# Up-projection of a two-layer decoder trunk: seven block products in place of eight on four K blocks of eight strip pairs per layer

## The chip, the cores and the metric

One NeuronCore of one Trainium2 chip runs the whole program. The metric is the device time of one execution in microseconds (us), lower being better. Below, PE is TensorE, DVE is VectorE, ACT is ScalarE, POOL is GpSimd and SP is SyncE; SP only starts transfers here, and POOL starts those of the turns described below.

## What is computed

The reference is a decoder trunk of two layers on 256 tokens of width 2048, all in float32. Each layer is an attention (stick-breaking in the first, dilated windows over a shared K and V in the second), then a gated feed-forward block, then a gated addition of a per-layer embedding. The change is in the feed-forward block only:

```python
def conv_ffn(h, w_up, conv_w, conv_b, w_down):
    u = causal_depthwise_conv(h @ w_up, conv_w, conv_b)
    gate, val = u[..., :D_FF], u[..., D_FF:]
    return (jax.nn.silu(gate) * val) @ w_down
```

Here `D_FF` is 5632, so `w_up` is 2048 by 11264, and the convolution runs over three tokens within a column.

## The kernel before

**Products.** Weights are cut into strips of 512 columns. K, the 2048 rows of `w_up`, is cut into 16 blocks of 128. A strip's product for the 256 tokens is two accumulators of 128 tokens by 512 columns, each one PSUM bank. Each block takes three matmuls for each accumulator, since both operands are held as a high and a low part: x low by w high, x high by w low, x high by w high (`add_block`, L336). So a strip is 16 blocks x 2 halves of the tokens x 3 = 96 matmuls of 128x512.

**Weights.** `weights` (L274) lets SP load four blocks at a time (one `raw` buffer, 1 MB, four such buffers in the pool). Two blocks together, a tile of 1024 columns, are then split: ACT writes the high part `whi` (L302), DVE subtracts it from the raw weights and writes `wlo` (L303). There are four buffers each of `whi` and `wlo`, so the splits can run up to four tiles ahead of PE. PE uses a tile in 12 matmuls.

**The feed-forward block.** `ffn` takes the up-projection in two parts per layer: strips 0 to 4, then a part of the down-projection, then strips 5 to 10, then the rest of the down-projection. Each strip s is a pair: the gate strip s and the value strip s + 11 (`products`, L356, called at L803). When a strip's accumulators are complete, ACT scales them out of PSUM (`scaled`, L406), DVE transposes 32 by 32 squares (L240), POOL sends the result through DRAM to finish the turn (L243, L251), and one strip later ACT and DVE do the convolution, the gate, and the split for the down-projection (L771 to L793, L147, L148).

**Order.** The order on each engine is fixed when the program is built: a scheduler places the instructions by priority, and every engine then takes its own list strictly in that order, waiting on semaphores. Weight splits are recorded with a higher priority (`high_priority`) so that they stand early. Matmuls stand in the order in which the code is written.

Of the kernel before, what the change touches and what calls it, by code (L numbers as in the profile page):

```python
# [26 lines left out]
FB = FF // P  # L27
# [45 lines left out]
def tile_trunk(ctx, tc, head_d, xT_d, x_d, pT_d, pos_d, vec_d, cst_d, csb_d, wqkv, wo_a, wkv, wq_b, wo_b, wup, wdn, wpg, wpp, gfin_d, out_d):  # L73
    nc = tc.nc
# [156 lines left out]
    def four(s):  # L231

        return tt(s, (P, 4 * S), tag="four", bufs=3)
# [84 lines left out]
    def strip_v(W, s, xs, base=0, tail=2, ringed=0, begun=None, ends=True, before=lambda k0: None, room=None, halved=False, ready=None):  # L318

        n = len(xs)
        ps = begun or [None] * (2 + halved)
        it = ready or weights(W, s, n, before=before, base=base, ringed=ringed)
        it = steps(it, n, 2 + halved, tail if ends else 0)
        for k, o, hi, lo in (g for group in it for g in group):
            if ps[o] is None:
                ps[o] = bank("accv", "acc") if room is None else room[:, o]
                if halved and o:  # L330
                    ps[o] = ps[o][:, :S]
            c = slice((o - 1) * S, o * S) if halved and o else slice(0, 512)
# [3 lines left out]
    def add_block(ps, x, t, hi, lo, first, final):  # L336
        xh = x[:, t * P : (t + 1) * P]
        xl = x[:, S + t * P : S + (t + 1) * P]
        nc.tensor.matmul(ps, xl, hi, start=first, stop=False)  # L339
        nc.tensor.matmul(ps, xh, lo, start=False, stop=False)  # L340
        nc.tensor.matmul(ps, xh, hi, start=False, stop=final)  # L341

    def two_strips(W, strips, xs, before, block):

# [11 lines left out]
    def products(jobs, xs, late=None, at=0, then={}, side=2):  # L356

        jobs = list(jobs)
        if late is not None:
            n = len(xs)

            def add():
                with tc.issue_after(last["high"]), tc.issue_after(last["low weights"]):
                    late()

            def before(k0):
                if k0 == at:
# [16 lines left out]
            ready = None  # L389
            if at is None:  # L390
                W, s, base = jobs[0]
                ready = list(weights(W, s, 4, base=base + n))
                add()
            for b, (W, s, base) in zip(begun, jobs):
                yield strip_v(W, s, xs[n:], base + n, begun=b, ready=ready)
                ready = None
            jobs = jobs[side:]
        for W, s, base in jobs:
            yield strip_v(W, s, xs, base)

    def scaled(ps, rc, room):

# [357 lines left out]
    def ffn(i, xs, late, rc):  # L760
        cv = V_CONV + i * 4 * 2 * FB

        def taps(r, j, n=1):
            c = cv + r * 2 * FB + j
            return vec[:, c : c + n]

        def conv_turned(j, z, y):

            runs = y.rearrange("p o (a r) -> p o a r", r=32)
            for o in range(4):  # L770
                nc.scalar.activation(runs[:, o], z[:, :, o], AF.Identity, scale=taps(2, j + o), bias=taps(3, j + o))  # L771
                for d in (1, 2):
                    c = runs[:, o, :, d:]
                    nc.vector.scalar_tensor_tensor(c, z[:, :, o, : 32 - d], taps(2 - d, j + o), c, op0=OP.mult, op1=OP.add)  # L774
            for d in (1, 2):
                over = tt("over", (P, 7, 4, 2), bufs=2)[:, :, :, :d]
                w = taps(2 - d, j, 4).unsqueeze(1).unsqueeze(3).to_broadcast([P, 7, 4, d])
                nc.vector.tensor_tensor(over, z[:, :7, :, 32 - d :], w, op=OP.mult)
                c = y.rearrange("p o (a r) -> p a o r", r=32)[:, 1:, :, :d]
                nc.vector.tensor_tensor(c, c, over, op=OP.add)  # L780

        def part(strips, late=None):

            gs = []
            gate = [None]

            def finish_strip(value, s, z):
                y = four("val" if value else "gate").rearrange("p (o c) -> p o c", o=4)
                conv_turned(4 * s + value * FB, z, y)
                if not value:  # L790
                    gate[0] = y
                    return nc.scalar.activation(y, y, AF.Silu).ins
                nc.vector.tensor_tensor(y, y, gate[0], op=OP.mult)  # L793
# [23 lines left out]
        half = FB // 4 // 2  # L817
        gs, late, _ = part(range(half), late)
# [221 lines left out]
```

## Time and profile before

| what | value |
|---|---|
| median of 3 runs | 2302.58 us (2302.34 to 2302.81) |
| span of the profiled execution | 2298.6 us |
| PE busy | 2286.6 us (99%), 10197 matmuls recorded |
| weight loads of PE (PEld) | 1893.6 us (82%) |
| DVE busy | 1514.4 us (66%) |
| ACT busy | 1257.3 us (55%) |
| POOL busy | 328.4 us (14%) |
| HBM traffic | 233 GB/s over the span |

The page of the profile gives one execution. The profiled execution's own time is known only as its span, from the first to the last instruction; the median of the runs lies 4.0 us above it. A group of instructions is written as line, engine, operation, output<-input, count, busy time and mean time of one; the last column is the time that the engine stood idle just ahead of such instructions, and what ended that wait. An engine's busy share counts instructions that are under way, so for PE, whose matmuls overlap, starts say more than durations.

### The profile page before, as it was taken

What the parts mean: (1) busy time and instruction counts of PE and PEld (TensorE: products, weight loads), DVE (VectorE), ACT (ScalarE), POOL (GpSimd) and SP (SyncE); (2) the same over time, 40 slices, a digit from 0 to 9 for tenths busy, and PEclk for the clock granted to TensorE, in tenths of its full rate; (3) what the DMA queues carried; (4) which work ended last, traced back from release to release, by engine and by line L of the source; (5) the groups of instructions that cost most, each with busy time, mean ns of one, the idle gap of its engine ahead of it and who ended that gap; (6) DMA issues with size and microseconds to landing.
All of it is one profiled execution on the core that took longest, in us unless ns stands there. A gap on an engine that the chain in (4) does not pass through costs nothing.

```text
span 2298.6 us, 27859 instructions
## 1 busy us (share of the span) xinstructions
PE 2286.6 (99%) x10197; PEld 1893.6 (82%) x10197; DVE 1514.4 (66%) x2205; ACT 1257.3 (55%) x1680; POOL 328.4 (14%) x575
## 2 busy tenths in 40 slices
PE   9999999999999999999999999999999999999998
PEld 7888888888888888888888888888888888888887
DVE  7666666676754767765677665767675476776565
ACT  6554555655534555644565554565553465554554
POOL 0311111111100111101111331211110011110100
PEclk9999999999999999999999999999999999999999
DMA  8777667767656677767577776777765577776763
GB/s 308 254 236 250 221 240 249 247 239 246 223 199 208 241 245 240 244 205 246 205 263 240 252 262 216 262 253 242 237 237 188 215 237 243 244 238 211 239 226 119
DMA packets 98346, 538.44 MB, mean 234 GB/s; under 512 B 16672, under 2 KB 17568, under 8 KB 46752
## 3 DMA queue, kind: packets, MB, share of 16 engines
q1 hardware_dynamic: 63360, 435.46, 54.2%
q0 software_dynamic: 32560, 95.98, 14.0%
q10 hardware_dynamic: 2288, 5.21, 0.6%
q8 instruction: 80, 1.31, 0.2%
q14 instruction: 58, 0.48, 0.1%
HBM read 486.52 MB, written 50.07 MB: 233 GB/s over the span
## 4 chain that ended last, share of the span: by engine, by line
PE 97%; DMA 1%; ACT 1%; DVE 0%; issue 0%; POOL 0%; SPq 0%; ACTq 0%; DVEq 0%; POOLq 0%
PE accv L340 32%; PE accv L341 31%; PE accv L339 31%; PE two L420 1%; PE two L341 0%; PE two L340 0%; PE two L339 0%; DMA turned<-there 0%; DMA there<-y 0%; PE keys L420 0%; ACT whi L302 0%; DVE wlo L303 0%; DMA vec<-in_head 0%; ACT h L140 0%; POOL turned L251 0%
## 5 line engine op out<-in xcount | busy, mean ns | idle before, releaser
L303 DVE TENSOR_TENSOR wlo<-raw,whi 128x1024 fp32r<-128x1024 f32 (+1 forms) x824 | 1001.7, 1216 | 696.0 <-ACT whi L302 694.9
L302 ACT ACTIVATE whi<-raw 128x1024 fp32r<-128x1024 f32 (+1 forms) x824 | 867.8, 1054 | 910.4 <-PE accv L341 886.7
L341 PE MATMUL accv<-whi,h 128*128 128x512 f32 x2328 | 905.3, 389 | 0.0
L339 PE MATMUL accv<-whi,h 128*128 128x512 f32 x2328 | 904.1, 388 | 0.9 <-ACT whi L302 0.6
L340 PE MATMUL accv<-wlo,h 128*128 128x512 f32 x2328 | 904.6, 389 | 0.1
L339 PEld LDWEIGHTS accv<-whi,h 128*128 128x128 f32 x2328 | 437.0, 188 | 92.0 <-ACT whi L302 1.3
L340 PEld LDWEIGHTS accv<-wlo,h 128*128 128x128 f32 x2328 | 437.0, 188 | 91.5 <-DVE wlo L303 1.4
L341 PEld LDWEIGHTS accv<-whi,h 128*128 128x128 f32 x2328 | 437.1, 188 | 89.6
L243 POOL DMA_DIRECT2D there<-y x162 | 91.7, 566 | 1305.5 <-DVE y L240 1288.5
L339 PE MATMUL accv<-whi,g 128*128 128x512 f32 x704 | 273.9, 389 | 0.0
L340 PE MATMUL accv<-wlo,g 128*128 128x512 f32 x704 | 273.9, 389 | 0.0
L341 PE MATMUL accv<-whi,g 128*128 128x512 f32 x704 | 273.9, 389 | 0.0
L251 POOL DMA_DIRECT2D turned<-there x324 | 190.0, 593 | 430.2 <-DMA there<-y 208.0
L339 PEld LDWEIGHTS accv<-whi,g 128*128 128x128 f32 x704 | 132.1, 188 | 27.5
L341 PEld LDWEIGHTS accv<-whi,g 128*128 128x128 f32 x704 | 132.1, 188 | 27.5
L340 PEld LDWEIGHTS accv<-wlo,g 128*128 128x128 f32 x704 | 132.1, 188 | 27.3
L240 DVE STREAM_TRANSPOSE y<-u 128x512 f32<-128x512 f32 x122 | 85.4, 703 | 1.8 <-DMA there<-y 1.4
L339 PE MATMUL accv<-whi,o 128*128 128x512 f32 x200 | 78.0, 390 | 0.0
L341 PE MATMUL accv<-whi,o 128*128 128x512 f32 x200 | 77.9, 390 | 0.0
L340 PE MATMUL accv<-wlo,o 128*128 128x512 f32 x200 | 77.8, 389 | 0.0
L406 ACT ACTIVATE u<-accv,rcol 128x512 f32<-128x512 f32 x102 | 69.2, 678 | 13.7 <-PE accv L341 13.7
L774 DVE SCALAR_TENSOR_TENSOR val<-turned,vec,val 128x248 f32<-128x248 f32 (+1 forms) x176 | 72.2, 462 | 0.0
(163 smaller groups left out, 1179.6 us busy)
## 6 DMA issues: line engine op xcount, KB each, us to landing
raw<-in_wup SPq DMA_DIRECT2D x176, 1024.0 KB, 5.1
raw<-in_wdn SPq DMA_DIRECT2D x88, 1024.0 KB, 4.8
there<-y POOLq DMA_DIRECT2D x171, 256.0 KB, 5.0
turned<-there POOLq DMA_DIRECT2D x324, 128.0 KB, 4.8
raw<-in_wqkv SPq DMA_DIRECT2D x40, 1024.0 KB, 6.6
raw<-in_wpg SPq DMA_DIRECT2D x32, 1024.0 KB, 4.8
raw<-in_wkv SPq DMA_DIRECT2D x24, 1024.0 KB, 5.3
raw<-in_wo_a SPq DMA_DIRECT2D x16, 1024.0 KB, 5.2
```

The source lines that it names most:

```text
L240: last["turned"] = nc.vector.transpose(y.rearrange("p (b o r) -> p o b r", b=4, o=4), strip.rearrange("p (o b c) -> p o b c", o=4, b=4)).ins
L243: nc.gpsimd.dma_start(there[t * P : (t + 1) * P], y)
L251: nc.gpsimd.dma_start(z[32 * b : 32 * b + 32].rearrange("p a o r -> p a (o r)"), back[b])
L302: last["high"] = nc.scalar.activation(hi[:, c], r, AF.Copy).ins
L303: last["low weights"] = nc.vector.tensor_tensor(lo[:, c], r, f32(hi[:, c]), op=OP.subtract).ins
L339: nc.tensor.matmul(ps, xl, hi, start=first, stop=False)
L340: nc.tensor.matmul(ps, xh, lo, start=False, stop=False)
L341: nc.tensor.matmul(ps, xh, hi, start=False, stop=final)
L406: last["out"] = nc.scalar.activation(u, ps[t], AF.Copy, scale=rc[:, t : t + 1]).ins
L420: run.append(nc.tensor.matmul(*args, skip_group_check=True, **kw).ins)
L774: nc.vector.scalar_tensor_tensor(c, z[:, :, o, : 32 - d], taps(2 - d, j + o), c, op0=OP.mult, op1=OP.add)
```

## The change

Strips 2, 3, 4 and 6 to 10 of each layer (eight gate-and-value pairs, 16 in the program) take their first four K blocks in another way. Take these four blocks as two rows of two blocks, the tokens as two halves, and the pair's two strips as two columns. Then the part of the product that they make is a 2x2 by 2x2 product of blocks, with each block product six matmuls. The plain way takes eight such products, 48 matmuls. The change takes seven, 42 matmuls, of sums and differences of blocks (the Winograd form of Strassen's scheme), and combines them.

- `block_sums`, once per layer, makes the four sums of token blocks and splits them: on DVE four adds and four subtractions of 256 columns and two splits of 512, on ACT two copies of 512.
- `Seven` handles a pair. `load` fetches the four blocks of both strips into two `raw` buffers. The seven products (`first` to `seventh`) each split a 1024-column weight operand as a plain tile is split (L445 and L446), so a pair has 7 splits for 4. The weight sums are four in-place adds on DVE (L439). ACT copies two accumulators to SBUF (L478, L485), and DVE makes four sums of 512 columns in PSUM (L495 to L498).
- The first four products of a pair are put among the tiles of the value strip of the pair before, in front of tiles 1, 3, 5 and 7 of eight, or 1, 2, 4 and 5 of six, counted from 0. The last three stand in the pair's own gate strip, in front of tiles 0, 1 and 3 of six.
- The accumulators c11 and c21 of the gate strip are the two banks of the tile `two`, of which there is one; c12 and c22 of the value strip are `seven`.
- The ring of 512-column buffers grows from 40 to 42.

The new lines count in the file after the change, in which the old L302 and L303 are L305 and L306, L339 to L341 are L342 to L344, L406 is L540, L771 to L793 are L905 to L927, L147 and L148 are L150 and L151, and L240 is L243.

```diff
+HEADS8, HEADS6, TAILS = (1, 3, 5, 7), (1, 2, 4, 5), (0, 1, 3)
...
-NRING, NRAW, NWSP = 40, 4, 4
+NRING, NRAW, NWSP = 42, 4, 4
...
+        def add(self, out, a, b):
+            with tc.high_priority(offset=AHEAD):
+                nc.vector.tensor_tensor(out, a, b, op=OP.add)
+
+        def parts(self, r):
+            hi = wsp.tile([P, 2, 512], F32R, tag="hi", name=nm("whi"))
+            lo = wsp.tile([P, 2, 512], F32R, tag="lo", name=nm("wlo"))
+            with tc.high_priority(offset=AHEAD):
+                last["high"] = nc.scalar.activation(hi, r, AF.Copy).ins
+                last["low weights"] = nc.vector.tensor_tensor(lo, r, f32(hi), op=OP.subtract).ins
+            return hi, lo
...
+        def first(self):
+            gates = two_banks()
+            self.c11, self.c21 = gates[:, 0], gates[:, 1]
+            self.c12, self.c22 = (bank("seven", "acc") for _ in range(2))
...
+            w = self.parts(self.b11)
+            self.t, self.u = self.b11, self.b12
+            self.add(self.t, self.b11, self.b12)
+            self.add(self.u, self.b12, self.b22)
+            self.product(self.c11, self.token(0, 0), w, True)
+            with tc.high_priority(offset=AHEAD):
+                nc.scalar.activation(self.p, self.c11, AF.Copy)
...
+        def fourth(self):
+            w = self.parts(self.t)
+            self.add(self.t, self.t, self.b21)
+            self.product(self.c22, self.sums[2], w, True)
+            with tc.high_priority(offset=AHEAD):
+                nc.vector.tensor_tensor(self.p, self.c22, self.p, op=OP.add)
+                nc.vector.tensor_tensor(self.c21, self.c21, self.p, op=OP.add)
+                nc.vector.tensor_tensor(self.c22, self.q, self.c21, op=OP.subtract)
+                nc.vector.tensor_tensor(self.c12, self.c12, self.p, op=OP.subtract)
+
+        def fifth(self):
+            self.product(self.c11, self.token(2, 0), self.parts(self.b21))
+
+        def sixth(self):
+            self.product(self.c21, self.token(2, 1), self.parts(self.t))
+
+        def seventh(self):
+            self.product(self.c12, self.sums[3], self.parts(self.b22))
...
+    def strip_among(W, s, xs, hooks, begun=None, base=0):
+        n = len(xs) - base
+        ps = begun or [bank("accv", "acc") for _ in range(2)]
+        it = weights(W, s, n, base=base)
+
+        def tiles():
+            for i in range(n // 2):
+                if i in hooks:
+                    hooks[i]()
+                yield next(it)
+
+        for k, o, hi, lo in (g for group in steps(tiles(), n, 2) for g in group):
+            add_block(ps[o], xs[base + k], o, hi, lo, k == 0 and not begun, k == n - 1, begun is not None)
+        return ps
...
-            ups = products([(wup[i], s + v * FB // 4, 0) for s in strips for v in range(2)], xs, late, None)
...
+                    base = 4 if now else 0
+                    tiles = (len(xs) - base) // 2
+                    yield strip_among(W, s, xs, now.go_on() if now else {}, now and [now.c11, now.c21], base)
+                    yield strip_among(W, v, xs, after.begin(tiles) if after else {}, now and [now.c12, now.c22], base)
+                    now = after
```

**The order at the border of two pairs.** On PE, where the value strip of strip 2 of the first layer ends and the gate strip of strip 3 begins, there stood before (with what each waits for):

```order
L339 MATMUL accv_3972<-whi_4081,h_3297 128x512
L340 MATMUL accv_3972<-wlo_4082,h_3297 128x512
L341 MATMUL accv_3972<-whi_4081,h_3297 128x512
L339 MATMUL accv_3972<-whi_4081,h_3300 128x512
L340 MATMUL accv_3972<-wlo_4082,h_3300 128x512
L341 MATMUL accv_3972<-whi_4081,h_3300 128x512
L339 MATMUL accv_4139<-whi_4135,h_2694 128x512 [waits Activation_49]
L340 MATMUL accv_4139<-wlo_4136,h_2694 128x512 [waits DVE_49]
L341 MATMUL accv_4139<-whi_4135,h_2694 128x512
```

The same place on PE after the change, where `seven_3643` is the value strip's second accumulator, `two_4051` the next pair's c11 and c21, and the L455 rows are the fifth product:

```order
L343 MATMUL seven_3643<-wlo_4174,h_3318 128x512
L344 MATMUL seven_3643<-whi_4173,h_3318 128x512
L455 MATMUL two_4051<-whi_4225,h_2700 128x512 [waits DVE_49,Activation_49]
L455 MATMUL two_4051<-wlo_4226,h_2700 128x512
L455 MATMUL two_4051<-whi_4225,h_2700 128x512
L455 MATMUL two_4051<-whi_4225,h_2703 128x512
L455 MATMUL two_4051<-wlo_4226,h_2703 128x512
L455 MATMUL two_4051<-whi_4225,h_2703 128x512
L342 MATMUL two_4051<-whi_4237,h_2862 128x512 [waits Activation_49]
```

The next strip's first matmul used to wait for its split weights alone. The fifth product's first matmul also waits for DVE, and the count in that wait is reached only with L497, the last of the four sums in PSUM. The fourth product, whose result these sums need, stands 12 matmuls (the value strip's last tile) ahead of the fifth.

DVE at this place before, from the gate of the strip that was turned last (L793):

```order
L793 TENSOR_TENSOR val_3922<-val_3922,gate_3748 128x1024
L303 TENSOR_TENSOR wlo_4066<-raw_4063,whi_4065 128x1024
L148 TENSOR_TENSOR g_3942<-val_3922,g_3942 128x256
L148 TENSOR_TENSOR g_3943<-val_3922,g_3943 128x256
L148 TENSOR_TENSOR g_3944<-val_3922,g_3944 128x256
L148 TENSOR_TENSOR g_3945<-val_3922,g_3945 128x256
L303 TENSOR_TENSOR wlo_4082<-raw_4063,whi_4081 128x1024
L303 TENSOR_TENSOR wlo_4136<-raw_4133,whi_4135 128x1024
```

And after the change; `wlo_4226` is the low part for the fifth product, `wlo_4254` that for the sixth, `seven_4053` the fourth product's result c22, `seven_4052` c12 and `two_4051` c21:

```order
L446 TENSOR_TENSOR wlo_4226<-raw_4029,whi_4225 128x1024
L927 TENSOR_TENSOR val_3992<-val_3992,gate_3824 128x1024
L306 TENSOR_TENSOR wlo_4238<-raw_4235,whi_4237 128x1024
L495 TENSOR_TENSOR part_4054<-seven_4053,part_4054 128x512
L446 TENSOR_TENSOR wlo_4254<-raw_4029,whi_4253 128x1024
L496 TENSOR_TENSOR two_4051<-two_4051,part_4054 128x512
L498 TENSOR_TENSOR seven_4052<-seven_4052,part_4054 128x512
L497 TENSOR_TENSOR seven_4053<-part_4054,two_4051 128x512
L306 TENSOR_TENSOR wlo_4264<-raw_4235,whi_4263 128x1024
L151 TENSOR_TENSOR g_4012<-val_3992,g_4012 128x256
```

The four sums have been put into DVE's list with the split `wlo_4254` between the first and the second of them. That split needs `whi_4253`, which goes into the buffer that the fourth product's weights held, so ACT can begin it only when the fourth product is done. The place reads alike at all 16 pairs.

More of the change, by code (lines that the diff above doesn't have):

```diff
@@ L334, in strip_v, with add_block @@
         return ps
-    def add_block(ps, x, t, hi, lo, first, final):
+    def add_block(ps, x, t, hi, lo, first, final, again=False):
         xh = x[:, t * P : (t + 1) * P]
         xl = x[:, S + t * P : S + (t + 1) * P]
-        nc.tensor.matmul(ps, xl, hi, start=first, stop=False)
-        nc.tensor.matmul(ps, xh, lo, start=False, stop=False)
-        nc.tensor.matmul(ps, xh, hi, start=False, stop=final)
+        nc.tensor.matmul(ps, xl, hi, start=first, stop=False, skip_group_check=again)
+        nc.tensor.matmul(ps, xh, lo, start=False, stop=False, skip_group_check=again)
+        nc.tensor.matmul(ps, xh, hi, start=False, stop=final, skip_group_check=again)
     def two_strips(W, strips, xs, before, block):
@@ L399, in products, with block_sums @@
             yield strip_v(W, s, xs, base)
+    def block_sums(xs):
+        f = four("whole").rearrange("p (k c) -> p k c", k=4)
+        for k in range(4):
+            nc.vector.tensor_tensor(f[:, k], f32(xs[k][:, :S]), f32(xs[k][:, S:]), op=OP.add)
+        (a11, a21), (a12, a22) = ((f[:, k : k + 2, :P], f[:, k : k + 2, P:]) for k in (0, 2))
+        m = four("sums").rearrange("p (q i c) -> p q i c", q=4, i=2)
+        nc.vector.tensor_tensor(m[:, 0], a21, a22, op=OP.subtract)
+        nc.vector.tensor_tensor(m[:, 1], a11, a21, op=OP.subtract)
+        nc.vector.tensor_tensor(m[:, 2], m[:, 0], a11, op=OP.subtract)
+        nc.vector.tensor_tensor(m[:, 3], m[:, 2], a12, op=OP.add)
+        out = []
+        for q in (0, 2):
+            hi, lo = (rt("sum", dt=F32R) for _ in range(2))
+            src = m[:, q : q + 2].rearrange("p q i c -> p (q i c)")
+            nc.scalar.activation(hi, src, AF.Copy)
+            nc.vector.tensor_tensor(lo, src, f32(hi), op=OP.subtract)
+            for j in range(2):
+                out.append([[t[:, (2 * j + i) * P : (2 * j + i + 1) * P] for t in (hi, lo)] for i in range(2)])
+        return out
@@ new lines, in tile_trunk, with __init__, product, load @@
+    class Seven:
+        def __init__(self, W, s0, s1, xs, sums):
+            self.strips = W, s0, s1
+            self.sums = sums
+            self.token = lambda k, t: [[xs[k + i][:, c + t * P : c + (t + 1) * P] for c in (0, S)] for i in range(2)]
+        def add(self, out, a, b):
[8 more added lines that the diff above has]
+            return hi, lo
+        def product(self, ps, left, w, first=False):
+            for i in range(2):
+                xh, xl = left[i]
+                hi, lo = w[0][:, i], w[1][:, i]
+                for j, (x, y) in enumerate(((xl, hi), (xh, lo), (xh, hi))):
+                    begins, ends = first and i == j == 0, first and i == 1 and j == 2
+                    nc.tensor.matmul(ps, x, y, start=begins, stop=ends, skip_group_check=True)
+        def load(self):
+            W, s0, s1 = self.strips
+            raws = []
+            for s in (s0, s1):
+                raw = wraw.tile([P, RAW, 512], F32, tag="raw", name=nm("raw"))
+                nc.sync.dma_start(raw, W[s, 0])
+                raws.append(raw)
+            (self.b11, self.b21), (self.b12, self.b22) = ((r[:, :2], r[:, 2:]) for r in raws)
+        def first(self):
+            gates = two_banks()
+            self.c11, self.c21 = gates[:, 0], gates[:, 1]
+            self.c12, self.c22 = (bank("seven", "acc") for _ in range(2))
+            both = tt("part", (P, 1024), tag="e", bufs=1)
+            self.p, self.q = both[:, :512], both[:, 512:]
+            w = self.parts(self.b11)
[5 more added lines that the diff above has]
+                nc.scalar.activation(self.p, self.c11, AF.Copy)
+        def second(self):
+            w = self.parts(self.t)
+            self.add(self.t, self.t, self.b22)
+            self.product(self.c12, self.sums[0], w, True)
+            with tc.high_priority(offset=AHEAD):
+                nc.scalar.activation(self.q, self.c12, AF.Copy)
+        def third(self):
+            self.product(self.c21, self.sums[1], self.parts(self.u), True)
+        def fourth(self):
+            w = self.parts(self.t)
+            self.add(self.t, self.t, self.b21)
+            self.product(self.c22, self.sums[2], w, True)
+            with tc.high_priority(offset=AHEAD):
+                nc.vector.tensor_tensor(self.p, self.c22, self.p, op=OP.add)
[8 more added lines that the diff above has]
+            self.product(self.c12, self.sums[3], self.parts(self.b22))
+        def begin(self, tiles):
+            do = [self.first, self.second, self.third, self.fourth]
+            self.hooks = {0: self.load, **dict(zip({8: HEADS8, 6: HEADS6}[tiles], do))}
+            return self.hooks
+        def go_on(self):
+            return dict(zip(TAILS, (self.fifth, self.sixth, self.seventh)))
@@ L802, in part, with up_strips @@
             waiting = None
-            ups = products([(wup[i], s + v * FB // 4, 0) for s in strips for v in range(2)], xs, late, None)
+            def up_strips():
+                W, now = wup[i], None
+                for j, s in enumerate(strips):
+                    v = s + FB // 4
+                    after = Seven(W, s + 1, v + 1, xs, sums) if (j or late is None) and s + 1 in strips else None
+                    if j == 0 and late is not None:
+                        yield from products([(W, s, 0), (W, v, 0)], xs, late, None)
+                        continue
+                    base = 4 if now else 0
[3 more added lines that the diff above has]
+                    now = after
+            ups = up_strips()
             for s in strips:
@@ L817, in ffn @@
         half = FB // 4 // 2
+        sums = block_sums(xs)
         gs, late, _ = part(range(half), late)
```

## The prediction

> **What bounds the kernel now.** I read the page first, then what PE waited for in the whole trace.
>
> ```profile
> PE 2286.6 (99%) x10197; PEld 1893.6 (82%) x10197; DVE 1514.4 (66%) x2205; ACT 1257.3 (55%) x1680; POOL 328.4 (14%) x575
> ```
> ```profile
> PE warm L122 <- DVE zero L119: 1.2, 1, 1.2
> PE accv L339 <- ACT whi L302: 0.6, 1, 0.6
> PE accv L339 <- DVE h L141: 0.3, 1, 0.3
> ```
>
> PE is never without work except for 2.1 us, none of it in an up-projection. So a matmul that goes is time saved, and any new wait of PE is time lost. Next, busy time by stretch, for two stretches of about one strip pair each:
>
> ```profile
> core 0: us, PE busy (x) PEld busy (x) DVE busy (x) ACT busy (x) POOL busy (x), PEclk, DMA share, GB/s
> 783.50:827.00 43.50, 43.50 (x193) 36.03 (x192) 31.38 (x49) 25.37 (x34) 6.96 (x12) 1.00 0.72 241
> 827.00:870.50 43.50, 43.50 (x193) 36.04 (x192) 31.37 (x49) 25.38 (x34) 6.96 (x12) 1.00 0.73 242
> ```
>
> Per pair DVE is busy 31.4 of 43.5 us, ACT 25.4, at full clock. Matmul starts, in order of time (57 rows, first and last shown):
>
> ```profile
> 429.66 0.39 PE L341 MATMUL accv<-whi,h 128*128 128x512 f32 x1
> ...
> 442.36 0.39 PE L340 MATMUL accv<-wlo,h 128*128 128x512 f32 x1
> ```
>
> 56 steps in 12.70 us make 0.2268 us a matmul; its own 0.39 us overlaps the next. A tile of 12 takes 2.72 us.
>
> **The gain.** A pair has 42 matmuls for 48. Six times 0.2268 is 1.36 us, 16 pairs make 21.8 us. Alone that gives 2302.6 - 21.8 = 2280.8.
>
> **What DVE and ACT get.** Prices are starts of instructions that stand back to back:
>
> ```profile
> 582.46 1.23 DVE L793 TENSOR_TENSOR val<-val,gate 128x1024 f32<-128x1024 f32 x1
> 583.61 1.22 DVE L303 TENSOR_TENSOR wlo<-raw,whi 128x1024 fp32r<-128x1024 f32 x1
> 584.74 1.43 DVE L148 TENSOR_TENSOR g<-val,g 128x256 fp32r<-128x256 f32 x4
> 586.11 1.23 DVE L303 TENSOR_TENSOR wlo<-raw,whi 128x1024 fp32r<-128x1024 f32 x1
> ```
> ```profile
> 1473.76 0.68 DVE L753 TENSOR_TENSOR x<-accv,x 128x512 f32<-128x512 f32 x1
> 1474.36 1.22 DVE L303 TENSOR_TENSOR wlo<-raw,whi 128x1024 fp32r<-128x1024 f32 x1
> ```
>
> A split takes DVE 1.13 us to the next start (1.22 to its own end), an in-place product of 1024 columns 1.15 (1.23), a sum of 512 columns out of PSUM 0.60 (0.68). A weight sum has the shape of that product, so I take its price. A sum that also writes PSUM is nowhere in the trace; its bounds are the 0.60 and 0.68 of the one that only reads it, and I take 0.60, as the others go by starts too. A pair adds three splits, four weight sums and four PSUM sums: 3 x 1.13 + 4 x 1.15 + 4 x 0.60 = 10.4 us. DVE then has 31.4 + 10.4 = 41.8 us in a pair in which PE has 186 x 0.2268 = 42.2 us. So DVE goes from 72% to 99% of PE's time. ACT's prices, read in the same way:
>
> ```profile
> 583.79 1.34 ACT L147 ACTIVATE g<-val 128x256 fp32r<-128x256 f32 x4 [1.00 <-DVE val L793]
> ...
> 595.33 1.06 ACT L302 ACTIVATE whi<-raw 128x1024 fp32r<-128x1024 f32 x1 [0.67 <-PE accv L341]
> 596.29 0.67 ACT L406 ACTIVATE u<-accv,rcol 128x512 f32<-128x512 f32 x1
> 596.86 1.57 ACT L771 ACTIVATE gate<-turned,vec 128x256 f32<-128x256 f32 x3
> ```
>
> Three splits and two copies are 3 x 0.96 + 2 x 0.57 = 4.0 us; with 25.4 ACT stays at 70%. Most of DVE's added work is hidden, since splits run up to four tiles ahead, but DVE has no room left to be early.
>
> **The wait that the change adds.** PE cannot begin the fifth product before the fourth of the four PSUM sums (L497) is done. Those sums need the fourth product, and between the two PE has one tile, 12 matmuls. How a chain from PE by ACT and DVE runs is in the chain of waits:
>
> ```profile
> 1441.33 0.24 PE accv L341
> 1441.57 0.02 issue
> 1441.59 1.07 ACT whi L302
> 1442.66 0.02 issue
> 1442.69 1.23 DVE wlo L303
> ```
>
> Let T be the fourth product's end. PE's next matmul starts at T - 0.16 (0.39 less 0.23), so PE is at the fifth at T - 0.16 + 2.72 = T + 2.56. On the other side, at the least: ACT's split for the sixth product reuses the fourth's buffer, so it runs from T + 0.02 to T + 1.09; DVE's part of it, which stands between the first two sums, starts at T + 1.12; then 1.13, two sums at 0.60, the last to its own end 0.68, and 0.04 to PE: T + 4.17. PE waits 1.6 us at the least.
>
> I take more, because the row ahead of the first sum is `wlo_4238`, which also waits for PE. Its high part reuses the buffer of the tile that ends 1.36 us ahead of T: ACT runs it to T - 0.27, DVE from T - 0.24 to T + 0.89. Then the first sum takes to T + 1.49, the split to T + 2.62, the sums to T + 3.82 and T + 4.50, and PE goes on at T + 4.54, after 2.0 us. ACT has two copies of `g` (0.34 us each) ahead of the sixth product's split; if they run from T - 0.27, it ends at T + 1.5 instead of T + 1.09, still in time.
>
> What one start after a wait costs, PE's last wait shows:
>
> ```profile
> 1481.97 0.39 PE L341 MATMUL accv<-whi,h 128*128 128x512 f32 x1
> 1482.67 0.50 PE L339 MATMUL accv<-whi,h 128*128 128x512 f32 x1 [0.32 <-DVE h L141]
> 1483.01 0.39 PE L340 MATMUL accv<-wlo,h 128*128 128x512 f32 x1
> 1483.23 0.40 PE L341 MATMUL accv<-whi,h 128*128 128x512 f32 x1
> ```
>
> The step after it is 0.34 for 0.23, 0.11 us more. So a pair loses 2.0 + 0.11 = 2.1 us and saves 1.36, a loss of 0.75 us. Behind the waiting matmul is queued the whole gate strip; ACT and DVE wait for its buffers in turn, and the next border finds them as this one did, so nothing is caught up. 16 x 0.75 = 12.0 us.
>
> **What I cost at nothing.** The first product of a pair writes the one tile `two`, which ACT must have emptied of the gate strip before. ACT first does a split that waits for the gate strip's last tile, then the two copies: 0.02 + 0.96 + 0.57 + 0.67 = 2.2 us after the gate strip's end, against the 2.56 us of the tile that covers it. It fits by 0.3 us; without that cover it is 2.2 us a pair. `block_sums` (eight operations like the 0.34 us steps of L148 and two splits of 512, some 4 us of DVE a layer) has a whole strip pair, over 40 us, before its first use, and stands behind the late blocks of the norm, not ahead. If it did delay PE it would cost 4 us twice. SP's list keeps its length and POOL's too, and loads are as many as before, but two of the four raw buffers are now held for most of a strip. A load takes:
>
> ```profile
> DMA to landing us min/median/max: 4.6/5.1/10.2
> ```
>
> A value strip of six tiles and four products lasts 6 x 2.72 + 4 x 1.36 = 21.8 us for three buffers, 7.3 each, so with two buffers a buffer's turn is 14.5 us. Of that go 5.1 for the load, 1.06 + 1.23 for its second split on ACT and DVE, and about 4.1 (a tile and a product) between its two splits: 3.0 us are spare, and loads cost nothing.
>
> **The sum.** The span is 2298.6, the median run 2302.6; the 4.0 us around the span stay. 2302.6 - 21.8 + 16 x 2.11 = 2314.6. The wait at its least (1.6, no restart) gives 2302.6 + 16 x 0.24 = 2306.4.
>
> **Rivals.**
>
> *The border is covered (not slower).* Were the sums in PSUM not held up by the split between them, they would be done at T + 0.02 + 3 x 0.60 + 0.68 + 0.04 = T + 2.54, just inside PE's 2.56, and the kernel would take 2281 to 2283. It decides at a wait of 1.25 us, where loss and gain are equal. For it speaks only that a sum in PSUM might be cheaper than 0.60; against it the order, which has the split between the sums at all 16 places. 4% for a gain over 0.2%, which is 4.6 us and about what a measurement of this kernel can tell; another 8% for a wait so near 1.25 us that the change is not told from none.
>
> *DVE is the bound.* At 99% by starts, DVE is over PE by durations: 7 x 1.22 + 4 x 0.68 = 11.3, so 42.7 us for PE's 42.2. Each pair then ends 0.9 us later than I said, 14 us in all: 2329. The rows above speak against it, as an instruction starts 0.09 us before the one ahead ends. [...] 14%.
>
> *Loads come late.* With two raw buffers, a load at the worst landing comes 5.1 us later, 3.0 of them spare, so 2.1 us reach PE by the splits and by the tile `two`. On half of the pairs that is 17 us: 2331. It decides at a landing of 8 us; the median speaks against it, the worst for it. 8%.
>
> *PE slows after the wait.* The kernel's first matmuls are slow:
>
> ```profile
> 1.20 3.87 PE L122 MATMUL warm<-zero 128*128 128x512 bf16 x9 [1.20 <-DVE zero L119]
> ```
>
> That is 0.43 us each, 0.20 over the later pace. If each wait brought this pace back for nine matmuls, it would cost 1.8 us a pair, 29 us: 2344. After the 0.3 us wait above the pace was back at the second step. [...] 2%.
>
> **The numbers.** My forecast has 64%, the border covered or nearly so 12%, DVE 14%, loads 8%, the slow pace 2%. The time is the forecast's, 2314.6. The range takes in the least wait and the cases of DVE and of late loads: 2304 to 2332; outside lie the covered border, the slow pace and part of the near cases. Faster 0.04, same 0.08, slower 0.88.
>
> **What would show it.** Right: PE at L455 waits for DVE L497 16 times, about 2.0 us each, 32 us in all, the next start 0.34 us on; 96 matmuls fewer at an unchanged 0.2268; DVE near 42 us a pair. The step on the chain is wrong if the first sum starts before T + 0.5 or if PE waits under 1.25 us; the step on loads or on `two` if PE waits at other rows of L455 or at L342; the pace if starts after the wait stay above 0.23. No wait of PE at the border would make the prediction wrong outright.

## The result, and the profile after

| | us, median (lowest to highest) | ratio to before, 95% interval |
|---|---|---|
| before, same chip | 2302.69 (2302.34 to 2303.03) | 1 |
| after | 2371.38 (2369.03 to 2381.09) | 1.0309 (1.0289 to 1.0330) |
| forecast | 2314.6 (2304 to 2332) | 1.005 |

Slower was right; the loss is 68.7 us where 12.0 were forecast, and outside the range. All comparisons, here and below, use undisturbed runs; the kernel called raw5w3 has only two of these and no interval.

Engine totals, from the page of the changed kernel:

```profile
span 2368.7 us, 27996 instructions
PE 2298.2 (97%) x10101; PEld 1891.0 (80%) x10101; DVE 1680.5 (71%) x2401; ACT 1319.6 (56%) x1764; POOL 328.7 (14%) x575
```

Ninety-six matmuls are gone, and DVE has 166.1 us more. Of these 8.2 are the sums of tokens (the kernel called plain, below, has them without the pairs and has DVE busy for 1522.6 us); the rest is 9.9 us a pair, near the forecast's 10.4. That DVE is busy 71% of the whole span does not show whether it is short of time within the pairs; the experiments do. What PE waited for, in us, number and longest:

```profile
PE two L455 <- DVE seven L497: 36.4, 16, 2.7
PE two L455 <- ACT u L540: 18.9, 11, 1.9
PE seven L343 <- DVE wlo L306: 2.9, 6, 0.8
PE warm L125 <- DVE zero L122: 1.2, 1, 1.2
PE accv L342 <- DVE h L144: 1.1, 1, 1.1
```

Before, these waits came to 2.1 us in all; now they come to 60.5. The first row is the border wait of the prediction, at all 16 places. The second and third were not in it: the first product of a pair waits for ACT to empty `two`, and a tile waits for its split. Behind both stands a row in what ACT waits for; in the kernel before ACT never waited for the up-projection's weights:

```profile
ACT whi L305 <- DMA raw<-in_wup: 72.4, 16, 7.2
```

The chain of waits shows how a load gets from there to PE (one stretch, in order of time: start, us, what):

```profile
483.33 10.50 DMA raw<-in_wup
...
493.93 1.07 ACT whi L305
...
495.02 1.24 DVE wlo L306
...
496.30 0.50 PE seven L343
...
499.73 1.26 ACT u L540 x2
...
501.02 2.25 PE two L455 x5
```

The load took 10.50 us where the median is 5.0; from its issue to its landing the DMA engines were 96% busy, at 307 GB/s. What went out ahead of it is in SP's list (start, duration until the last issue, count):

```profile
471.56 0.33 SPq L288 DMA_DIRECT2D raw<-in_wup  x1
474.49 7.66 SPq L462 DMA_DIRECT2D raw<-in_wup  x2
483.33 5.67 SPq L288 DMA_DIRECT2D raw<-in_wup  x2
```

The pair's two loads stand on SP ahead of the value strip's own first load. The second of the two got a buffer only at 481.8, so the load that the value strip needs first went out last, 1.5 us behind another one of 1 MB. ACT begins nothing while the split that wants it waits, 6.54 us; the two copies that empty `two` come behind that split, at 499.73:

```profile
486.33 1.06 ACT L305 ACTIVATE whi<-raw 128x1024 fp32r<-128x1024 f32 x1 [0.49 <-PE two L344]
493.93 1.06 ACT L305 ACTIVATE whi<-raw 128x1024 fp32r<-128x1024 f32 x1 [6.54 <-DMA raw<-in_wup]
...
498.76 1.06 ACT L445 ACTIVATE whi<-raw 128x1024 fp32r<-128x1024 f32 x1 [1.87 <-DVE raw L439]
499.73 1.25 ACT L540 ACTIVATE u<-two,rcol 128x512 f32<-128x512 f32 x2
```

The third thing is what PE does after a border wait, in order of time:

```profile
471.13 0.39 PE L344 MATMUL accv<-whi,h 128*128 128x512 f32 x1
473.48 0.47 PE L455 MATMUL two<-whi,h 128*128 128x512 f32 x1 [1.96 <-DVE seven L497]
...
475.69 0.63 PE L342 MATMUL two<-whi,h 128*128 128x512 f32 x1
476.12 0.63 PE L343 MATMUL two<-wlo,h 128*128 128x512 f32 x1
...
477.66 0.39 PE L344 MATMUL two<-whi,h 128*128 128x512 f32 x1
477.89 0.40 PE L342 MATMUL two<-whi,h 128*128 128x512 f32 x1
```

From 474.0 the steps are 0.43 for 0.23, and from 477.4 they are short again. The granted clock (PEclk, third from the right) says the same of the two stretches:

```profile
470.00:473.50 3.50, 1.54 (x8) 0.99 (x6) 3.50 (x6) 2.64 (x4) 0.00 (x0) 1.00 0.50 166
473.50:477.50 4.00, 4.00 (x11) 3.13 (x12) 3.01 (x5) 2.71 (x5) 1.13 (x2) 0.57 0.93 352
```

The trace's clock record has 14 such periods, each 3.413 us at half clock, between the first up-projection and the last. Every one starts within 1.4 us of the end of one of these waits, and all starts are whole multiples of 3.413 us apart. Nine of them follow border waits and five follow waits of the first product. One costs half its length, 1.71 us of work: 14 x 1.71 = 23.9 us.

**The sum of the profiled execution**, by terms that are used again below: the span grew by 2368.7 - 2298.6 = 70.1. Saved matmuls -21.8; PE's waits 60.5 - 2.1 = 58.4; half-clock periods 23.9; and 0.27 for each of 32 waits more than before, 8.6 (0.11 for the restart, as forecast, and 0.16 because the wait column counts from the end of the last 0.39 us matmul, of which 0.23 is its step). Together 69.1.

### The profile page after: what moved, and what is told of

Same layout as the page of the kernel before. It is cut to its first block, busy times and chain, and to the rows that moved or that the text cites. A ratio compares the mean times of both kernels' runs of the same rounds, so it can differ in the third digit from the quotient of the medians.

```text
span 2368.7 us, 27996 instructions
## 1 busy us (share of the span) xinstructions
PE 2298.2 (97%) x10101; PEld 1891.0 (80%) x10101; DVE 1680.5 (71%) x2401; ACT 1319.6 (56%) x1764; POOL 328.7 (14%) x575
## 4 chain that ended last, share of the span: by engine, by line
PE 79%; DVE 11%; DMA 5%; issue 2%; ACT 2%; POOL 0%; DVEq 0%; ACTq 0%
PE accv L342 21%; PE accv L343 21%; PE accv L344 21%; DMA raw<-in_wup 5%; DVE wlo L306 4%; DVE wlo L446 3%; PE two L455 3%; PE two L342 2%; PE two L343 2%; PE two L344 2%; PE seven L343 2%; PE seven L344 2%; PE seven L342 2%; PE two L554 1%; ACT whi L305 1%
## 5 line engine op out<-in xcount | busy, mean ns | idle before, releaser
L306 DVE TENSOR_TENSOR wlo<-raw,whi 128x1024 fp32r<-128x1024 f32 (+1 forms) x760 | 922.2, 1215 | 574.0 <-ACT whi L305 572.9
L305 ACT ACTIVATE whi<-raw 128x1024 fp32r<-128x1024 f32 (+1 forms) x760 | 800.1, 1054 | 820.1 <-PE accv L344 581.5
L342 PE MATMUL accv<-whi,h 128*128 128x512 f32 (+1 forms) x1304 | 506.4, 388 | 1.1 <-DVE h L144 1.1
L344 PE MATMUL accv<-whi,h 128*128 128x512 f32 (+1 forms) x1304 | 507.4, 389 | 0.0
L343 PE MATMUL accv<-wlo,h 128*128 128x512 f32 (+1 forms) x1304 | 506.6, 388 | 0.0
L342 PEld LDWEIGHTS accv<-whi,h 128*128 128x128 f32 x1304 | 245.2, 188 | 51.9 <-ACT whi L305 2.0
L343 PEld LDWEIGHTS accv<-wlo,h 128*128 128x128 f32 x1304 | 245.3, 188 | 50.5 <-DVE wlo L306 0.2
L344 PEld LDWEIGHTS accv<-whi,h 128*128 128x128 f32 x1304 | 245.3, 188 | 50.1
L342 PE MATMUL accv<-whi,g 128*128 128x512 f32 x704 | 273.9, 389 | 0.0
L344 PE MATMUL accv<-whi,g 128*128 128x512 f32 x704 | 273.9, 389 | 0.0
L445 ACT ACTIVATE whi<-raw 128x1024 fp32r<-128x1024 f32 x112 | 118.4, 1058 | 102.3 <-PE two L344 33.3
L446 DVE TENSOR_TENSOR wlo<-raw,whi 128x1024 fp32r<-128x1024 f32 x112 | 136.7, 1221 | 26.3 <-ACT whi L445 26.0
L343 PE MATMUL seven<-wlo,h 128*128 128x512 f32 x384 | 152.0, 396 | 2.9 <-DVE wlo L306 2.9
L342 PEld LDWEIGHTS accv<-whi,g 128*128 128x128 f32 x704 | 132.2, 188 | 27.6
L344 PEld LDWEIGHTS accv<-whi,g 128*128 128x128 f32 x704 | 132.2, 188 | 27.5
L342 PE MATMUL two<-whi,h 128*128 128x512 f32 x384 | 153.3, 399 | 0.0
L343 PE MATMUL two<-wlo,h 128*128 128x512 f32 x384 | 152.4, 397 | 0.0
L342 PE MATMUL seven<-whi,h 128*128 128x512 f32 x384 | 151.9, 396 | 0.0
```

The source lines that it names most:

```text
L305: last["high"] = nc.scalar.activation(hi[:, c], r, AF.Copy).ins
L306: last["low weights"] = nc.vector.tensor_tensor(lo[:, c], r, f32(hi[:, c]), op=OP.subtract).ins
L342: nc.tensor.matmul(ps, xl, hi, start=first, stop=False, skip_group_check=again)
L343: nc.tensor.matmul(ps, xh, lo, start=False, stop=False, skip_group_check=again)
L344: nc.tensor.matmul(ps, xh, hi, start=False, stop=final, skip_group_check=again)
L445: last["high"] = nc.scalar.activation(hi, r, AF.Copy).ins
```

## Experiments

My theory after the result: three causes make the loss. (A) The border wait, a chain longer than its cover. (B) A load issued in the wrong order, which reaches PE by ACT's queue. (C) Half-clock periods that follow waits of some 1.9 us. Rivals: DVE is the bound after all and waits only show where; the rewritten loop costs something itself; the clock falls for another reason. The kernel before took 2300.8 to 2300.9 on the chips of these runs. Ratios are to it.

**plain**: every pair by eight products again.

```diff
-                    after = Seven(W, s + 1, v + 1, xs, sums) if (j or late is None) and s + 1 in strips else None
+                    after = None
```

> All pairs by eight products again; the rest of the rewritten loop and the four sums of tokens per layer stay. My theory puts the whole loss on the seven products' own waits (55.3 us of PE's idle time at L455) and on the half-speed clock periods that follow them (14 of about 1.7 us): so 2302 to 2304, no half-clock period, no wait of PE in an up-projection. Rival, the rewritten loop and the sums of tokens cost something of their own: 2306 or more.

2300.20, ratio 0.9994 (0.9982 to 1.0007), like the kernel before on this chip, both somewhat under the 2302 to 2304 expected; no half-clock period, no wait in an up-projection. The loop and the sums of tokens are free; the loss is all the seven products'.

**heads**: A. The fourth product stands one tile earlier at all 16 pairs; in value strips of six tiles, which host 12 of them, the added line moves the third product one tile earlier too.

```diff
-HEADS8, HEADS6, TAILS = (1, 3, 5, 7), (1, 2, 4, 5), (0, 1, 3)
+HEADS8, HEADS6, TAILS = (1, 3, 5, 6), (1, 2, 3, 4), (0, 1, 3)
```

> The fourth product one tile earlier, so that two tiles (5.4 us) and not one (2.7 us) lie between it and the fifth. Theory, the wait at the border is a chain's length against its cover: the chain of 4.5 to 5.2 us fits, PE's wait for L497 falls from 36.4 us to under 3, nine of the fourteen half-clock periods go with it, and the time falls by about 36 + 4 (restarts) + 9 x 1.7 = 55 to some 2316, if the waits for the tile two (18.9 us) stay as they are. Rival, DVE is the bound: the waits only move to other rows and the time stays above 2360. Rival, the half-clock periods do not come from the waits: 2371 - 40 = 2331 with about 14 periods left.

2307.12, ratio 1.0022 (1.0011 to 1.0033), 9 us below the theory's figure. What PE waited for in it:

```profile
PE two L455 <- ACT u L540: 8.5, 6, 1.9
PE seven L343 <- DVE wlo L306: 2.6, 4, 0.8
...
PE two L455 <- DVE seven L497: 1.1, 2, 0.6
```

The border wait went from 36.4 to 1.1 and three half-clock periods are left. The loads' part shrank too, from 18.9 to 8.5, which I had not expected; so this edit is not A alone, and whether the earlier third product did it was not tried. DVE does the same work (1673.3 us) in 65 us less: it is not the bound.

**load**: B alone. At the head of a pair the value strip's own first tile is fetched ahead of the call that loads the pair's weights.

```diff
             for i in range(n // 2):
+                tile = next(it) if i == 0 else None
                 if i in hooks:
                     hooks[i]()
-                yield next(it)
+                yield tile or next(it)
```

> At the head of a pair the value strip's own first load is issued ahead of the pair's two loads; the fourth product stays where the change has it. Theory, ACT's queue is held by the one load that was issued last of three in 9 us (10.5 us to land): with that load ahead of the pair's two, ACT's waits for raw weights fall from 72.4 us under 40, PE's waits for the tile two from 18.9 under 8, L497's stay at 34 to 38: 2371 less 11 to 20, 2350 to 2360. Rival, what counts is that two buffers are held, whatever the order: then the pair's own loads come late instead, PE waits at the first product for L446 or L445, and the time stays at 2365 to 2378.

2326.01, ratio 1.0103 (1.0083 to 1.0123): 24 us below the best that the theory gave. SP's list at the same place, to be set beside the one above:

```profile
470.03 3.26 SPq L288 DMA_DIRECT2D raw<-in_wup  x2
478.71 1.84 SPq L462 DMA_DIRECT2D raw<-in_wup  x2
485.56 0.33 SPq L288 DMA_DIRECT2D raw<-in_wup  x1
```

The value strip's load now goes out by 473.3, not at 483.3, and the pair's two follow together. PE's only wait there of more than 0.2 us:

```profile
PE two L455 <- DVE seven L497: 32.7, 16, 2.6
```

All waits for ACT to empty `two` are gone. Of the 16 border waits 13 are now 1.96 us (1.97 in one of them), near the forecast's 2.0, and 10 of 14 half-clock periods are gone, more than the five that the expectation for raw5w3 counted on: only four of these waits have 1.9 us or more within one period of 3.413 us, the others are cut by its boundary. What was wrong was the order of the loads, not the holding of two buffers, which this kernel does as well; the longest landing is still 11.0 us, but PE no longer waits behind a load. ACT's waits for raw weights fell from 72.4 us to

```profile
ACT whi L305 <- DMA raw<-in_wup: 8.9, 5, 3.0
```

**raw5w3** and **w3**: B from another side, first with five raw buffers and three pairs of split tiles, then three pairs alone (`42, 4, 3` in the added line).

```diff
-NRING, NRAW, NWSP = 42, 4, 4
+NRING, NRAW, NWSP = 42, 5, 3
```

> Five buffers for raw weights instead of four, paid for with three instead of four pairs of split tiles. Theory, the first product of a pair comes late because two of four raw buffers are held and loads bunch: with three free buffers no load lands later than about 7 us, ACT's waits for raw weights (72.4 us) fall under 20, PE's waits for the tile two (18.9 us) fall under 6 and up to five half-clock periods go: 2345 to 2355, if three split tiles are enough elsewhere. If they are not, PE shows waits for L305 and L306 that it did not have. Rival, DVE is the bound: the waits of PE keep their sum, 2365 to 2375.

> Three pairs of split tiles, four raw buffers: the other half of the kernel with five raw buffers. Theory, the fifth raw buffer took away the late loads and nothing else did: here PE's waits for the tile two and for L306 stay at 15 us or more (or grow, as splits run less far ahead and free raw buffers later), and the time is 2350 to 2385. Rival, the fewer split tiles were what helped, by another order on ACT and DVE: waits and time like those with five raw buffers, 2326 to 2332.

raw5w3 took 2328.02 and 2329.55, at least 15 us less than expected; w3 2369.35, ratio 1.0299 (1.0273 to 1.0326). PE's waits with five raw buffers:

```profile
PE two L455 <- DVE seven L497: 20.4, 16, 2.0
PE seven L343 <- DVE wlo L306: 3.2, 4, 1.0
```

and with four:

```profile
PE two L455 <- DVE seven L497: 20.4, 16, 2.0
PE seven L342 <- ACT whi L305: 17.4, 10, 3.0
PE seven L343 <- DVE wlo L306: 14.2, 24, 0.8
```

Three split pairs put another order on DVE (in w3 the first sum starts 0.24 us after the fourth product's end at places like 524.9 us, for 0.91 at the earliest in the changed kernel), which shortens the border wait to 20.4 in both and was no part of my theory. What the fifth raw buffer adds is that the value strip's splits are no longer late: 31.6 us of waits become 3.2, the half-clock periods in the up-projections fall from ten to three, and 41 us of time go. I had expected no landing over 7 us; the longest was 11.3. The loads land no faster (median 5.6 us, 5.7 in w3), but ACT's waits for them are 9.5 us for 65.8.

**warm**: eight matmuls on unused data ahead of each first and each fifth product, into a bank that nobody reads.

```diff
+    def keep_warm():
+        ps = bank("warm")
+        for _ in range(IDLE):
+            nc.tensor.matmul(ps, cbf[:, :P], cbf[:, :512], start=True, stop=True)
...
         def first(self):
...
             self.c12, self.c22 = (bank("seven", "acc") for _ in range(2))
+            keep_warm()
...
         def fifth(self):
+            keep_warm()
             self.product(self.c11, self.token(2, 0), self.parts(self.b21))
```

> Eight matmuls on unused data (1.8 us) ahead of each fifth product and each first product, 32 places, into a bank that nobody reads; nothing else. They add 58 us of work, of which PE's present waits there hide about 54. Theory, the clock halves because PE stands idle for 1.9 us or more: the half-clock periods vanish (0 to 2 left), the granted clock is 0.997 or more, and the time is 2371 - 24 + 6 to 12 = 2353 to 2360. Rival, the periods have another cause (power, the clock's own rhythm): some 14 remain and the time is 2376 to 2384.

2375.61, ratio 1.0318 (1.0280 to 1.0355): the time is nearly as the rival had it, the trace is between. Its two largest waits (rows one helper further down, so L462 is the after kernel's L455):

```profile
PE two L462 <- DVE seven L505: 16.1, 11, 2.4
PE accv L349 <- DVE h L151: 5.6, 2, 5.1
```

The second row is not at a pair: its longest wait, 5.1 us, ends at 1519 us, ahead of the second layer's first pair. Five half-clock periods are left, each after a wait of 1.92 us or more, that one included; elsewhere they went with the waits, which the theory of C asks for. The time did not fall because the dummies cost more than I allowed: 256 x 0.2268 = 58.1 us went in, and only about 33 us of waits came out. By the terms above: -21.8 + 58.1 + (27.7 - 2.1) + 5 x 1.71 + 20 x 0.27 = 75.9; the span grew by 77.2.

**loadsum**: load, and DVE's split for the sixth product is issued after the last sum in program order (L498); `parts` holds its DVE half behind the instruction that it is given.

```diff
-                self.product(self.c21, self.token(2, 1), self.parts(self.t))
+                self.product(self.c21, self.token(2, 1), self.parts(self.t, self.sum))
```

> As the kernel with the load moved, the fourth product where the change has it, but DVE's split for the sixth product is held behind the four sums in PSUM instead of standing between the first two. Theory, that split is 1.13 us of the border's chain: PE's wait for L497's sum falls from 32.7 us to 14 to 20 in all (about 0.9 to 1.2 at each of 16 borders), the four half-clock periods go, and the time falls from 2326 to 2300 to 2308. Rival, the wait only moves to the sixth product, which then waits for its split: 2320 to 2328.

2309.97, ratio 1.0040 (1.0026 to 1.0054), 16 us less than load; the theory's direction, short of its size: the border waits sum to 24.1 us for the 14 to 20 expected, and three half-clock periods stay. PE's waits (this kernel's L456 and L498 are the after kernel's L455 and L497):

```profile
PE two L456 <- DVE seven L498: 18.3, 11, 2.9
PE two L456 <- ACT whi L305: 5.8, 5, 1.2
```

At four borders the wait is 0.95 us where load has 1.96: the split between the sums was on the chain, as the prediction said. No wait went to the sixth product. At five borders the fifth product now waits 1.16 us, by the profile for ACT's L305, and at seven 1.57 to 2.91 us for DVE; at the longest DVE has the convolution's last product (L929, 1.22 us) and a split right ahead of the sums.

**heads53**: heads with raw5w3.

```diff
+HEADS8, HEADS6, TAILS = (1, 3, 5, 6), (1, 2, 3, 4), (0, 1, 3)
+NRING, NRAW, NWSP = 42, 5, 3
```

> Both at once: the fourth product one tile earlier, and five raw buffers with three pairs of split tiles. Theory, the two causes are separate and add up: of the waits that the earlier fourth product left (11.1 us for the tile two and for splits late after a load, three half-clock periods of 1.7) nearly all go with the fifth raw buffer, so 2307 less 15 to 22: 2285 to 2292, faster than the kernel before on the same chip by 0.4 to 0.7%. Rival, DVE, now 74% busy, sets the end: not under 2300. Rival, three pairs of split tiles are too few with two products so close together: new waits of PE for L446 and L306 of 10 us or more, 2300 or more.

2332.65, ratio 1.0131 (1.0112 to 1.0151): a miss, 25 us worse than heads. The second rival was right; the waits are spread over ten rows, of which the two largest are

```profile
PE seven L343 <- DVE wlo L306: 10.2, 12, 1.0
PE seven L455 <- DVE wlo L446: 4.3, 7, 0.8
```

Eight of the ten are waits for splits: with products in neighbouring tiles three split pairs don't let splits run far enough ahead. The waits do not account for all of the loss (see the terms below).

**headtail**: heads, and the seventh product one tile earlier.

```diff
+HEADS8, HEADS6, TAILS = (1, 3, 5, 6), (1, 2, 3, 4), (0, 1, 2)
```

> The fourth product one tile earlier and the seventh too, so that the second raw buffer of a pair is let go one tile (2.7 us) earlier; four raw buffers. Theory, the remaining waits for the tile two (8.5 us) and for late splits (4.1) come from held raw buffers: ACT's waits for raw weights fall from 35 us to under 20, the time from 2307 to 2296 to 2302. Rival, the buffers are let go too late in any case: 2305 to 2309.

2300.63, ratio 0.9994 (0.9984 to 1.0005), 6.5 us below heads, within the range expected: ACT's waits for raw weights fell from 35.2 us to 15.9. PE's waits that were to go with them fell less (for `two` from 8.5 us to 5.8, for the splits not at all); of the gain 3.4 us are two half-clock periods.

**headload** and **headloadtail**: heads and load together (below); the second has headtail's line in place of heads'.

```diff
+HEADS8, HEADS6, TAILS = (1, 3, 5, 6), (1, 2, 3, 4), (0, 1, 3)
...
+                tile = next(it) if i == 0 else None
                 if i in hooks:
                     hooks[i]()
-                yield next(it)
+                yield tile or next(it)
```

> Both edits that worked, each against its own wait: the fourth product one tile earlier (border) and the value strip's own load ahead of the pair's two (loads); four raw buffers, four pairs of split tiles. Theory, with both causes gone little but the saved matmuls is left: PE's waits in the up-projections sum to under 5 us, no half-clock period or one, and the time is 2301 - 21.8 + 2 to 6 = 2281 to 2286, faster than the kernel before by 0.65 to 0.85%. Rival, DVE at 73% is close enough to a bound, or ACT's queue finds another late load: 2290 to 2300.

> As headload, and the seventh product one tile earlier. Theory, the second raw buffer of a pair comes free 2.7 us earlier, which matters only if loads still come late in headload: then up to 3 us less than headload, otherwise the same within 2 us. Rival, three products in three tiles one behind the other ask more of ACT and DVE than they give in time: 3 us more than headload or worse.

headload took 2280.73, ratio 0.9912 (0.9899 to 0.9926), headloadtail 2279.98, ratio 0.9911 (0.9897 to 0.9924). Both beat the kernel before by 0.9%, and they can't be told apart. headload's largest wait:

```profile
PE two L455 <- DVE seven L497: 3.4, 6, 1.3
```

No half-clock period is left in either. Of headload's page, to be set beside that of the changed kernel:

```profile
span 2283.2 us, 28012 instructions
PE 2267.3 (99%) x10101; PEld 1875.4 (82%) x10101; DVE 1678.3 (74%) x2401; ACT 1318.3 (58%) x1764; POOL 327.7 (14%) x575
```

The same 10101 matmuls and the same work on DVE take 85.5 us less. How close DVE comes within a pair shows in a stretch of headloadtail, columns as in the prediction:

```profile
819.50:864.00 44.50, 44.50 (x197) 36.72 (x196) 43.36 (x65) 31.05 (x41) 6.94 (x12) 1.00 0.67 237
```

DVE is busy 97% of it and PE all of it: DVE was nearly full, as forecast, and still not the bound.

**The terms over the kernels** (profiled executions; growth of the span over before's 2298.6; waits less before's 2.1; 1.71 for a period; 0.27 for a wait; -21.8 in each):

| | waits | periods | growth by the terms | measured |
|---|---|---|---|---|
| after | 58.4 (32 more) | 14 | 69.1 | 70.1 |
| load | 32.2 (16 more) | 4 | 21.5 | 21.4 |
| loadsum | 26.1 (17 more) | 3 | 14.0 | 14.1 |
| heads | 14.1 (14 more) | 3 | 1.2 | 4.9 |
| headtail | 11.9 (14 more) | 1 | -4.4 | -2.9 |
| headload | 4.0 (8 more) | 0 | -15.6 | -15.4 |
| headloadtail | 0.8 (1 more) | 0 | -20.7 | -20.2 |

Five of seven agree within 1 us. What makes heads' 3.7 us and headtail's 1.5 stays open. In the three kernels with three split pairs (w3, raw5w3, heads53) the span grew by 14 to 16 us more than the terms say. About 7.8 of these lie behind PE's last matmul, where no wait of PE can show them: it starts 17.9 to 18.0 us before the end in these three, 10.1 to 10.2 in all other kernels. The rest stays open.

## Why the prediction was wrong

**The gain and the prices were right.** 96 matmuls fewer at an unchanged step; DVE 9.9 us a pair more for 10.4; a sum in PSUM 0.69 us to its own end and 0.60 to the next start. headloadtail, with next to no new wait, gives back 20.8 of the 21.8 us.

**The border was right in mechanism and 7 us short in size.** The fourth product's end T is 468.80 at the place shown above. The first sum began at 469.71 (T + 0.91, forecast 0.89), L497 ended at 473.33 (T + 4.53, forecast 4.50), PE went on 0.15 us after that for the forecast's 0.04, and the wait came out at 1.96 in nine of 16 places. The end of the fourth product and DVE's list behind it:

```profile
468.41 0.39 PE L455 MATMUL seven<-whi,sum 128*128 128x512 f32 x1
```

```profile
468.57 1.23 DVE L306 TENSOR_TENSOR wlo<-raw,whi 128x1024 fp32r<-128x1024 f32 x1 [0.68 <-ACT whi L305]
469.71 0.68 DVE L495 TENSOR_TENSOR part<-seven,part 128x512 f32<-128x512 f32 x1
470.31 1.22 DVE L446 TENSOR_TENSOR wlo<-raw,whi 128x1024 fp32r<-128x1024 f32 x1
471.44 0.69 DVE L496 TENSOR_TENSOR two<-two,part 128x512 f32<-128x512 f32 x1
472.05 0.69 DVE L498 TENSOR_TENSOR seven<-seven,part 128x512 f32<-128x512 f32 x1
472.64 0.69 DVE L497 TENSOR_TENSOR seven<-part,two 128x512 f32<-128x512 f32 x1
```

At the other seven it was 2.65 to 2.71: there DVE has no pause ahead of the sums (a split, the product of value and gate L927 and another split run right up to them), and the first sum starts later, at T + 1.51 to T + 1.56. My chain had DVE free at T - 0.24 everywhere. On the prediction's measure (0.16 above the wait column) the borders cost 36.4 + 16 x 0.16 = 39.0 us for 31.7. That the split between the sums belongs to the chain is shown by loadsum. My rival of a covered border left out the other split, which in my own chain holds the first sum until T + 0.89: with only the split between the sums gone, loadsum still waits 0.95 us at its best borders.

**"It fits by 0.3 us" and "loads cost nothing" failed: 26 us.** (18.9 + 2.9 + 17 x 0.27.) I worked out a steady state with two free buffers, 3.0 us to spare; ACT's 16 waits for raw weights, one to a pair, fit that between the heads of pairs. At the head of a pair there is none to spare: SP's list puts two loads that nobody needs yet ahead of the one that is needed next, and with buffers held the second of them waits for one and blocks the load behind it. I noted that SP's list "keeps its length", which is true and was the wrong question; its order changed. My rival on late loads had the path right (splits, then `two`), but as a matter of a long landing on half of the pairs; the condition was the order of issue, and one moved load took away all of it. With that load in time, in load, no first product waits for ACT to empty `two`, so the fit by 0.3 us was sound in itself and failed only behind a late split.

**The full pace behind a 2.0 us wait failed: 24 us.** The slow pace is the rival that I gave 2%. The forecast counted nothing for the pace behind the border wait. No run shows that as true of waits of 2.0 us in general; what the changed kernel's trace showed in its place is 14 periods at half clock behind waits of 1.91 to 2.71 us, at 1.71 us each (I had written 1.8 a pair), though after nine of the 16 borders and five of the first product's waits, not after every border. I had taken the one wait of 0.3 us in the trace before as evidence against a slow pace; it was too short to tell anything: in the changed kernel too no half clock followed a period with under 1.70 us idle.

**"DVE is the bound" (14%) was wrong**, as forecast: with the same work the time ranges from 2280 to 2371. Its price was also mis-worked: 42.7 us of DVE fit into the 44.3 us (42.2 + 2.1) that a pair lasts by the forecast, so 0.9 us more a pair did not follow. That rival added the durations up; in the changed kernel's trace the sum behind a split starts 0.09 us before the split's recorded end (471.44 for the split of 470.31 and 1.22).

So 12.0 forecast, + 7 at the border, + 26 by the loads, + 24 by the clock make 69. What the experiments add is that these don't come apart cleanly: the late loads lengthened PE's waits and moved them on the clock's grid, so the one edit of load took 10 half-clock periods away with them.

## What to carry to other kernels

When a change adds loads that are held, look at the order of the issuing queue at the place where they enter, not at the mean time per buffer: here the load that was needed next stood behind one that waited for a buffer until 481.8, the split that wanted it kept ACT idle for 6.54 us, and through ACT's list such loads made PE wait 18.9 us for `two`; with one load moved, in load, these waits were gone. A new wait of PE is priced with its clock: here a wait of 1.96 us within one period of the grid cost 3.7 us (1.96 + 1.71), and waits that left under 1.70 us in each period brought no half clock. A change that saves little per step and adds one dependence, as here 1.36 us against a chain of 4.5, is decided by where the steps stand; give the chain a cover longer than itself before judging the idea (in heads, with two tiles or 5.4 us as the cover, the border waits fell from 36.4 us to 1.1).

## What was new about the hardware

In these traces PE's clock changes in periods of 3.413 us on a fixed grid. I added up PE's idle time (by the wait column) within each period from 340 us on in nine traces, after, heads, warm, raw5w3, w3, heads53, load, loadsum and headtail. Periods with 1.9 us idle or more were followed by a period at half clock in all 35 cases, those with 1.70 to 1.87 in 4 of 13, those under 1.70 in none, except that in w3 four stretches at half clock lasted for two periods. So a wait of 1.96 us that falls into one period costs 1.71 more (half of 3.413, an estimate from the recorded clock of 0.5), and one of 2.66 that a boundary cuts into 1.31 and 1.35 (at 963 us in the changed kernel) costs nothing more. That idle time is the cause is shown only as far as the periods went with the waits in heads, load and warm; a wait of set length was not tried. What decides between 1.70 and 1.87 stays open.
